# A transformer trunk on one core: the memory's projections begin earlier and run denser in the attention, and the top-k masks are built another way

## The chip, the core and the metric

The kernel runs on one core of one Trainium2 chip. The metric is the device time of one execution in microseconds, the median of several runs. The core has four engines that matter here: TensorE (PE, matrix products and transposes), VectorE (DVE), ScalarE (ACT) and GpSimd (POOL). Each works through its own instructions in a fixed order and waits on semaphores for the others. SyncE (SP) issues all the transfers in one queue.

## What is computed

Two layers of an encoder for 1024 tokens of width 1024. A layer is a mixer (a short convolution, an attention whose keys are picked by an indexer, an attention over a band of chunks), then a cross-attention into 256 memory tokens, then a squared-ReLU MLP, each with a residual and a layer norm.

```
for l in range(DEPTH):                       # 2
    mix = hybrid_mixer(x, positions, w_in[l], conv_w[l], rel_bias[l], w_mix_out[l])
    x = layer_norm(ALPHA * x + mix, ...)
    cross = memory_cross_attention(x, mem, w_mq[l], w_mkv[l], w_mo[l])
    x = layer_norm(ALPHA * x + cross, ...)
    x = layer_norm(ALPHA * x + squared_relu_mlp(x, w_ff1[l], w_ff2[l]), ...)

# in hybrid_mixer, the attention with picked keys (dsa), block of 128 queries:
score = einsum('bqh,bqhs->bqs', iw, relu(einsum('bqhd,bsd->bqhs', iq, ik)))
score = where(admissible, score, -inf)
_, idx = lax.top_k(score, 256)               # ties: the lowest index first
s = where(valid, q . k[idx] * scale, -inf);  out = softmax(s) . v[idx]

# in memory_cross_attention, from mem alone:
k, v = split(einsum('bmd,de->bme', mem, w_kv), 2)
```

## The kernel before

The products are made in three matmuls each, from operands that are split into a high and a low part: `mm3`, lines 340 to 342. A weight unit of 512 columns is loaded by a transfer (line 284), its high part is cast on ACT (285) and its low part subtracted on POOL (286).

A layer has these stages in order of time. First the projections of the token stream and, beside them, the indexer and a bitwise search for each query's 256th largest score (`topk`; line 788 on ACT and 792 on DVE count how many scores exceed a candidate). Then **the attention**: 24 units of the chunk attention (6 heads by 4 pairs of blocks, 48 softmax rows of 128 queries) and 16 units of the dsa attention (8 blocks `b` by 2 halves of the heads, 48 softmax rows). A softmax row's scores are made on PE (line 1088 for chunk, 1220 for dsa, two matmuls a pass), one or two passes of DVE add bias or mask and take the minimum (988), ACT makes the exponential (994), POOL divides (1005), PE transposes (1125, 1240), ACT and DVE split (644, 645), and PE multiplies by the values (1139, 1249). A unit's values come three units behind its scores (`pipeline`, `LEAD = 3`). A dsa unit needs its block's mask, which `masks` makes for blocks 2 to 7; wider blocks have wider rows, up to 1024 keys.

Into the attention three streams are merged (`merge`, at the end of `back`): the units, the mask steps, and `memory`, which computes for the cross-attention what depends on the memory tokens alone: for each of 4 heads the keys, the values, and the values times the output weights (stored to DRAM by line 1412). Per layer that is 384 matmuls of 256 columns and 96 of 512. Each stream advances by numbers that it yields; `after(START, RATE, ...)` delays `memory` to the moment 30 and stretches its steps by 2.0. The attention's units sum to some 158 of these moments, and `memory`'s steps to 62.4 before they are stretched. The order so written is a priority; a scheduler that works with a model of the chip then fixes every engine's order when the program is built.

After the attention comes the output projection (`out_proj`), whose 16 weight units are `w_mix_out`; then the cross-attention, its projection and the MLP.

Of the kernel before, what the change touches and what calls it, by code (L numbers as in the profile page):

```python
# [15 lines left out]
BF16 = mybir.dt.bfloat16  # L16
I32 = mybir.dt.int32
AF = mybir.ActivationFunctionType
ALU = mybir.AluOpType
# [3 lines left out]
S = 1024  # L23
# [9 lines left out]
TOPK = 256  # L33
# [4 lines left out]
BIG = 2.0**100  # L38
# [8 lines left out]
ROOMY = 8192  # L47
FILL = 200
TP = 2.5
START = 30  # L50
RATE = 2.0
EARLY = 0
STEP = 32
STAGES = 4
# [256 lines left out]
class Kern:  # L311
# [508 lines left out]
    def masks(self, st):  # L820

        nc, sb = self.nc, self.sb
        while "found" not in st:
            yield 1.0
        state, col = st.pop("found")
        for g, blocks in list(enumerate(GROUPS))[::-1]:
            fl, cnt = state[g][0], state[g][2]
            for j, b in list(enumerate(blocks))[::-1]:
                w = (b + 1) * P
                sc = st["score"][b]  # L830
                tcol = fl[:, j : j + 1]
                tmp = [sb.alloc(w) for _ in range(2)]
                eq, pre = (x.ap for x in tmp)
                if g == 0:


                    above, more = self.small(1), self.small(1)
                    nc.vector.tensor_scalar(
                        eq, sc.ap, tcol, None, op0=ALU.is_gt, op1=ALU.add,
                        accum_out=cnt[:, j : j + 1],  # L840
                    )
                    nc.vector.tensor_scalar(
                        eq, eq, -HIGH, HIGH, op0=ALU.mult, op1=ALU.add
                    )
                    nc.vector.tensor_tensor_reduce(
                        pre, sc.ap, eq, 1.0, HIGH, op0=ALU.add, op1=ALU.min,
                        accum_out=above,
                    )
                    nc.vector.tensor_scalar(
                        more.bitcast(I32), cnt[:, j : j + 1], float(TOPK), None,  # L850
                        op0=ALU.is_ge,
                    )
                    nc.vector.copy_predicated(tcol, more.bitcast(I32), above)

                nc.vector.tensor_scalar(
                    eq, sc.ap, tcol, BIG, op0=ALU.is_equal, op1=ALU.mult
                )
                nc.vector.tensor_scalar(
                    sc.ap, sc.ap, tcol, None, op0=ALU.is_le, op1=ALU.add,
                    accum_out=cnt[:, j : j + 1],  # L860
                )
                need = self.small(1)
                nc.vector.tensor_scalar(
                    need, cnt[:, j : j + 1], float(TOPK - w), BIG, op0=ALU.add, op1=ALU.mult
                )
                nc.vector.tensor_tensor_scan(pre, eq, eq, 0.0, op0=ALU.add, op1=ALU.max)
                nc.vector.scalar_tensor_tensor(
                    eq, pre, need, eq, op0=ALU.is_le, op1=ALU.mult
                )
                nc.vector.scalar_tensor_tensor(  # L870
                    sc.mask, sc.ap, BIG, eq, op0=ALU.mult, op1=ALU.subtract
                )
                for x in [sc.high] + tmp:
                    sb.free(x, self.w.late)
                st["masks"].add(b)
                yield 7.5
        sb.free(col, self.w.late)
# [1100 lines left out]
    def build(self):  # L1978
# [14 lines left out]
        for l in range(DEPTH):  # L1993
# [16 lines left out]
            def attention():  # L2010
                yield from self.pipeline(units())
                for x in ("dkT", "dv"):
                    sb.free(st.pop(x))

            def back():
# [20 lines left out]
                def mask_steps():  # L2036
                    for d in st["mask steps"]:
                        yield 2.0 * d

                yield from self.merge(  # L2040
                    attention(), mask_steps(),
                    self.after(START, RATE, self.shift(FILL, self.memory(l, st))),
                )
# [99 lines left out]
```

## Time and profile before

| | |
|---|---|
| median of 3 runs | 3014.02 us (3011.82 to 3014.43) |
| profiled execution | 3010.65 us, of which its span is 3008.8 us |
| PE busy in the span | 2884.2 us (96%) |
| DVE, ACT, POOL busy | 2155.3 (72%), 1558.0 (52%), 1299.5 us (43%) |
| attention of layer 1, layer 2 | from 297 to 572 us, from 1786 to 2062 us of the span |

PE's busy time is the union of its matmuls' durations; matmuls overlap in the pipeline, so a busy PE can still do little. The first softmax pass of a layer starts its attention; the last matmul of line 1249 is near its end. Shares of the other engines are true occupancy.

### The profile page before, as it was taken

Reading aid. Unit: us, or ns where it says so; the run is one execution under the profiler, and the core shown is the slowest. Engines: PE = TensorE matmul, PEld = TensorE weight load, DVE = VectorE, ACT = ScalarE, POOL = GpSimd, SP = SyncE. Lnnn points to the kernel's source line nnn. Section 1 sums busy time; section 2 is a strip of 40 time slices with the busy share of each in tenths; the row PEclk is TensorE's granted clock in tenths of the full one; section 3 lists DMA queues with packets and bytes.
Section 4 is the critical chain, followed back from the end, with each engine's and each line's share of the span. In section 5 each row is a group of like instructions: output and inputs, shape, how many; then the busy total and the mean of one; then the engine's idle time right before and its main releaser. Section 6 shows DMA issues by size and latency. Waiting matters only on the chain. (4 is left out here: it accounts for less than half of the span.)

```text
span 3008.8 us, 43448 instructions
## 1 busy us (share of the span) xinstructions
PE 2884.2 (96%) x14440; PEld 2440.8 (81%) x14440; DVE 2155.3 (72%) x4321; ACT 1558.0 (52%) x3146; POOL 1299.5 (43%) x1242
## 2 busy tenths in 40 slices
PE   8999889999999999999999998899999999999998
PEld 7787778788877788888788877887888778888886
DVE  5897786582487766777857987866625877667788
ACT  5676777623234455543457767784222445554432
POOL 4614575522335553222457146653222555532223
PEclk9999999999999999999999999999999999999999
DMA  4213333331334546755422144232213354476553
GB/s 127 63 36 85 101 110 106 105 119 36 114 116 161 171 154 217 255 178 188 131 68 66 37 100 118 92 117 97 93 47 111 112 175 163 152 250 223 189 179 116
DMA packets 264288, 381.99 MB, mean 127 GB/s; under 512 B 23040, under 2 KB 141824, under 8 KB 264064
## 3 DMA queue, kind: packets, MB, share of 16 engines
q1 hardware_dynamic: 264064, 379.22, 38.7%
q8 instruction: 114, 1.87, 0.3%
q14 instruction: 110, 0.90, 0.1%
HBM read 269.56 MB, written 95.42 MB: 121 GB/s over the span
## 5 line engine op out<-in xcount | busy, mean ns | idle before, releaser
L340 PE MATMUL banks<-sb,sb 128*128 128x512 f32 (+3 forms) x3776 | 1423.0, 378 | 19.7 <-DVE sb L645 6.3
L341 PE MATMUL banks<-sb,sb 128*128 128x512 f32 (+3 forms) x3776 | 1417.7, 376 | 8.6 <-POOL sb L286 8.6
L342 PE MATMUL banks<-sb,sb 128*128 128x512 f32 (+3 forms) x3776 | 1413.9, 376 | 7.7 <-POOL sb L645 7.4
L645 POOL TENSOR_TENSOR sb<-sb,sb 128x512 fp32r<-128x512 f32 (+1 forms) x428 | 590.1, 1390 | 931.3 <-ACT sb L644 793.5
L340 PEld LDWEIGHTS banks<-sb,sb 128*128 128x128 f32 x3776 | 714.3, 189 | 151.4 <-DVE sb L645 9.1
L342 PEld LDWEIGHTS banks<-sb,sb 128*128 128x128 f32 x3776 | 712.7, 189 | 133.2 <-POOL sb L645 9.2
L341 PEld LDWEIGHTS banks<-sb,sb 128*128 128x128 f32 x3776 | 714.4, 189 | 130.8 <-POOL sb L286 10.3
L644 ACT CAST sb<-sb 128x512 fp32r<-128x512 f32 (+1 forms) x788 | 452.8, 605 | 583.5 <-PE banks L341 146.2
L286 POOL TENSOR_TENSOR sb<-sb,sb 128x512 fp32r<-128x512 f32 (+2 forms) x288 | 381.4, 1340 | 480.1 <-ACT sb L285 421.2
L645 DVE TENSOR_TENSOR sb<-sb,sb 128x512 fp32r<-128x512 f32 x360 | 273.2, 785 | 43.8 <-ACT sb L644 41.4
L645 DVE TENSOR_TENSOR sb<-banks,sb 128x384 fp32r<-128x384 f32 (+2 forms) x324 | 188.0, 595 | 86.4 <-ACT sb L644 78.9
L285 ACT CAST sb<-sb 128x512 fp32r<-128x512 f32 (+2 forms) x288 | 170.4, 606 | 136.1 <-PE banks L342 30.4
L644 ACT CAST sb<-banks 128x384 fp32r<-128x384 f32 (+2 forms) x324 | 159.7, 517 | 140.5 <-PE banks L1557 75.3
L792 DVE TENSOR_SCALAR_CACHE_REDUCE sb<-sb,sb 128x768 bf16<-128x768 f32 (+3 forms) x256 | 207.5, 810 | 5.0 <-POOL sb L443 2.0
L1721 DVE TENSOR_TENSOR sb<-sb,sb 128x512 f32<-128x512 f32 x160 | 155.5, 1006 | 60.9 <-ACT sb L1701 56.9
L1005 POOL TENSOR_SCALAR sb<-sb,sb 128x128 f32<-128x128 f32 (+7 forms) x192 | 148.2, 786 | 86.4 <-DVE sb L1003 65.9
L1763 DVE TENSOR_TENSOR sb<-banks,sb 128x512 f32<-128x512 f32 x224 | 149.4, 682 | 47.4 <-PE banks L342 45.7
L788 ACT ACTIVATE sb<-sb,sb 128x1024 bf16<-128x1024 f32 (+1 forms) x128 | 140.4, 1097 | 74.2 <-DVE sb L811 64.9
L1826 DVE TENSOR_TENSOR sb<-sb,sb 128x512 f32<-128x512 f32 x128 | 112.8, 882 | 68.4 <-DMA sb<-w_ff_dram 68.0
L994 ACT ACTIVATE sb<-sb,sb 128x128 f32<-128x128 f32 (+7 forms) x192 | 141.6, 739 | 27.9 <-DVE sb L988 26.5
L1700 ACT ACTIVATE sb<-sb 128x512 f32<-128x512 f32 x128 | 80.7, 631 | 117.6 <-DVE sb L1763 117.1
L1333 DVE SCALAR_TENSOR_TENSOR sb<-sb,banks 128x512 f32<-128x512 f32 x64 | 43.4, 685 | 113.2 <-PE banks L342 110.5
(172 smaller groups left out, 3046.9 us busy)
## 6 DMA issues: line engine op xcount, KB each, us to landing
sb<-h SPq DMA_DIRECT2D x236, 256.0 KB, 3.1
h<-sb SPq DMA_DIRECT2D x224, 256.0 KB, 2.2
sb<-w_ff_dram SPq DMA_DIRECT2D x216, 256.0 KB, 3.1
sb<-w_ff_dram SPq DMA_DIRECT2D x64, 512.0 KB, 4.1
sb<-w_in_dram SPq DMA_DIRECT2D x64, 256.0 KB, 2.9
sb<-w_mkv_dram SPq DMA_DIRECT2D x64, 256.0 KB, 2.8
sb<-sb SPq DMA_DIRECT2D x54, 256.0 KB, 3.6
xs<-sb SPq DMA_DIRECT2D x24, 512.0 KB, 2.8
```

What stands on the lines that cost most here:

```text
L285: k.nc.scalar.copy(hi, st)
L286: k.nc.gpsimd.tensor_tensor(lo, st, hi.bitcast(F32), op=ALU.subtract)
L340: mm(out, lh, rh, start=start, stop=False)
L341: mm(out, lh, rl, start=False, stop=False)
L342: mm(out, ll, rh, start=False, stop=stop)
L644: nc.scalar.copy(hi, src)
L645: eng.tensor_tensor(lo, src, hi.bitcast(F32), op=ALU.subtract)
L792: nc.vector.tensor_scalar(junkb[:, :w], x, c, None, op0=ALU.is_ge, op1=ALU.add, accum_out=n)
L994: nc.scalar.activation(pt.ap, pt.ap, AF.Exp, bias=mn, scale=-1.0, accum_out=sm)
L1005: nc.gpsimd.tensor_scalar(pt.ap, pt.ap, rc[:, i : i + 1], 0.0, op0=ALU.mult, op1=ALU.add)
L1721: nc.vector.tensor_tensor(z.ap, x, y, op=ALU.add if spec[1] == "+" else ALU.subtract)
L1763: nc.vector.tensor_tensor(r.ap, ps.ap, part[c, x].ap, op=ALU.add)
```

## The change

Two numbers: `memory` starts at the moment 10 in place of 30, and its steps are stretched by 1.1 in place of 2.0, so it ends at about 79 in place of 155. And the end of `masks`: before, DVE compares the scores for equality and for less-or-equal with the threshold, each over the whole row, scans the equal ones, and combines in two more passes. Now ACT writes the sign of threshold minus score (-1, 0, 1, as bf16, with its sum), DVE compares the sign with zero, scans, and combines in two passes; `need` takes one more instruction on one column.

```
-START = 30
-RATE = 2.0
+START = 10
+RATE = 1.1
...
+                side, same = (eq.bitcast(BF16)[:, i * w : (i + 1) * w] for i in range(2))
+                total, need = self.small(1), self.small(1)
+                nc.scalar.activation(
+                    side, sc.ap, AF.Sign, bias=tcol, scale=-1.0, accum_out=total
+                )
+                nc.vector.tensor_scalar(same, side, 0.0, None, op0=ALU.is_equal)
+                nc.vector.tensor_tensor_scan(pre, same, same, 0.0, op0=ALU.add, op1=ALU.max)
+
                 nc.vector.tensor_scalar(
-                    eq, sc.ap, tcol, BIG, op0=ALU.is_equal, op1=ALU.mult
+                    need, pre[:, w - 1 : w], total, 0.5, op0=ALU.add, op1=ALU.mult
+                )
+                nc.vector.tensor_scalar(need, need, float(TOPK - w // 2), None, op0=ALU.add)
+                nc.vector.scalar_tensor_tensor(
+                    pre, side, 4.0 * S, pre, op0=ALU.mult, op1=ALU.add
                 )
                 nc.vector.tensor_scalar(
-                    sc.ap, sc.ap, tcol, None, op0=ALU.is_le, op1=ALU.add,
-                    accum_out=cnt[:, j : j + 1],
-                )
-                need = self.small(1)
-                nc.vector.tensor_scalar(
-                    need, cnt[:, j : j + 1], float(TOPK - w), BIG, op0=ALU.add, op1=ALU.mult
-                )
-                nc.vector.tensor_tensor_scan(pre, eq, eq, 0.0, op0=ALU.add, op1=ALU.max)
-                nc.vector.scalar_tensor_tensor(
-                    eq, pre, need, eq, op0=ALU.is_le, op1=ALU.mult
-                )
-                nc.vector.scalar_tensor_tensor(
-                    sc.mask, sc.ap, BIG, eq, op0=ALU.mult, op1=ALU.subtract
+                    sc.mask, pre, need, BIG, op0=ALU.is_gt, op1=ALU.mult
                 )
```

What that does to the order is seen at three places. PE, layer 1, chunk attention: the place of the first projection matmuls of `memory` (340 to 342, 256 columns) among score passes (1088). Before, they stand behind 84 matmuls of line 1088:

```order
L1088 MATMUL banks<-sb_2839,sb_2815 128x320
L1088 MATMUL banks<-sb_2839,sb_2817 128x320
L340 MATMUL banks<-sb_331,sb_652 128x256
L341 MATMUL banks<-sb_2629,sb_652 128x256
L342 MATMUL banks<-sb_331,sb_652 128x256
```

Now they stand behind 38 of them:

```order
L1088 MATMUL banks<-sb_2620,sb_2608 128x320
L1088 MATMUL banks<-sb_2620,sb_2610 128x320
L1139 MATMUL banks<-sb_2919,sb_2629 128x256
L1139 MATMUL banks<-sb_2919,sb_2629 128x128
L340 MATMUL banks<-sb_2816,sb_652 128x256
L341 MATMUL banks<-sb_2818,sb_652 128x256
L342 MATMUL banks<-sb_2816,sb_652 128x256
```

So the projections begin with the twentieth score pass in place of the forty-third. PE, layer 2, dsa attention, block 5 (scores 1220, transposes 1240, values 1249), with `memory`'s products of 512 columns among them before:

```order
L1220 MATMUL banks<-sb_2610,sb_16370 128x384 x2
L1249 MATMUL banks<-sb_3450,sb_2608 128x384
L340 MATMUL banks<-sb_1821,sb_2813 128x512
L341 MATMUL banks<-sb_1821,sb_2813 128x512
L342 MATMUL banks<-sb_1821,sb_2813 128x512
L340 MATMUL banks<-sb_629,sb_2813 128x512
L341 MATMUL banks<-sb_629,sb_2813 128x512
L342 MATMUL banks<-sb_629,sb_2813 128x512
L1220 MATMUL banks<-sb_2610,sb_16370 128x384 x2
L1249 MATMUL banks<-sb_16732,sb_2608 128x384
```

The same place now:

```order
L1220 MATMUL banks<-sb_2610,sb_16887 128x384 x2
L1249 MATMUL banks<-sb_2762,sb_2620 128x384
L1220 MATMUL banks<-sb_2610,sb_16696 128x384 x2
L1249 MATMUL banks<-sb_5505,sb_2620 128x384
L1249 MATMUL banks<-sb_5399,sb_2620 128x384
L1249 MATMUL banks<-sb_5204,sb_2620 128x384
L1249 MATMUL banks<-sb_17042,sb_2620 128x384
L1220 MATMUL banks<-sb_2610,sb_16696 128x384 x2
```

No projection matmul is left among the scores and values. Counted over the program, of the 480 projection matmuls of a layer's `memory`, 240 (layer 1) and 246 (layer 2) stand behind the 60th softmax row before (192 of 256 columns, 48 and 54 of 512), and none now. POOL, end of layer 2's attention: the last divisions (1005), then weight units of the output projection (286) and splits of the attention's result (645). Before:

```order
L1005 TENSOR_SCALAR sb_4126<-sb_4126,sb_2662 128x1024
L1005 TENSOR_SCALAR sb_1671<-sb_1671,sb_2662 128x1024
L286 TENSOR_TENSOR sb_666<-sb_97,sb_666 128x512
L645 TENSOR_TENSOR sb_5639<-sb_14346,sb_5656 128x512
L645 TENSOR_TENSOR sb_5639<-sb_1761,sb_5656 128x512
L286 TENSOR_TENSOR sb_1837<-sb_102,sb_1837 128x512
L645 TENSOR_TENSOR sb_5639<-sb_16340,sb_5656 128x512 x2
```

Now:

```order
L1005 TENSOR_SCALAR sb_1761<-sb_1761,sb_2662 128x1024
L1005 TENSOR_SCALAR sb_163<-sb_163,sb_2662 128x1024
L286 TENSOR_TENSOR sb_2618<-sb_97,sb_2618 128x512
L286 TENSOR_TENSOR sb_2818<-sb_102,sb_2818 128x512
L286 TENSOR_TENSOR sb_659<-sb_107,sb_659 128x512
L286 TENSOR_TENSOR sb_652<-sb_112,sb_652 128x512
L286 TENSOR_TENSOR sb_317<-sb_97,sb_317 128x512
```

Eight weight units of the output projection now stand right behind the last division, where one stood before the first split.

## Rows read from the trace of the kernel before

**Rows 1.** The page, part 1: busy time and share of the span of one engine.
```profile
PE 2884.2 (96%) x14440; PEld 2440.8 (81%) x14440; DVE 2155.3 (72%) x4321; ACT 1558.0 (52%) x3146; POOL 1299.5 (43%) x1242
```

In the rows of stretches the columns are: stretch (us from the start of the span), its length, busy time of PE, PEld (weight loads), DVE, ACT and POOL with the number of instructions, PEclk (the clock granted to TensorE as a share of its full speed), the busy share of the transfer engines, GB/s. Rows of one line alone show only the engines that run it.

**Rows 2.** Busy us of each engine (count) in stretches of attention; columns below.
```profile
296.90:443.40 146.50, 127.49 (x851) 114.45 (x851) 118.09 (x339) 106.19 (x259) 89.23 (x102) 0.92 0.38 107
443.40:529.30 85.90, 84.20 (x570) 75.44 (x569) 60.30 (x170) 69.47 (x159) 52.97 (x62) 1.00 0.34 109
529.30:572.00 42.70, 40.00 (x234) 33.61 (x233) 32.57 (x72) 35.51 (x74) 15.08 (x13) 1.00 0.23 78
1785.70:1929.90 144.20, 126.55 (x848) 112.94 (x848) 118.93 (x335) 105.98 (x261) 92.73 (x105) 0.93 0.39 108
1929.90:2019.20 89.30, 85.28 (x583) 77.59 (x581) 63.75 (x176) 71.55 (x160) 54.54 (x61) 1.00 0.35 112
2019.20:2062.00 42.80, 37.30 (x210) 30.07 (x209) 33.13 (x75) 34.06 (x71) 17.61 (x15) 0.96 0.22 77
```

**Rows 3.** TensorE in order of time, consecutive projection matmuls: start, duration.
```profile
506.40 0.28 PE L341 MATMUL banks<-sb,sb 128*128 128x256 f32 x1
506.52 0.28 PE L342 MATMUL banks<-sb,sb 128*128 128x256 f32 x1
```

**Rows 4.** All engines in two stretches without a projection matmul.
```profile
300.00:350.00 50.00, 41.70 (x253) 36.95 (x254) 44.83 (x136) 38.60 (x94) 26.01 (x35) 0.86 0.31 91
2025.00:2040.00 15.00, 13.53 (x77) 10.56 (x75) 11.82 (x31) 13.03 (x27) 7.08 (x6) 1.00 0.05 19
```

**Rows 5.** The score passes, line 988 alone, in chosen stretches: VectorE busy, count.
```profile
300.00:350.00 50.00, 17.16 (x70) 0.86 0.31 91
350.00:420.00 70.00, 16.87 (x66) 0.98 0.46 127
440.00:520.00 80.00, 24.81 (x86) 1.00 0.36 115
1790.00:1835.00 45.00, 15.71 (x64) 0.92 0.36 100
1835.00:1905.00 70.00, 16.01 (x64) 0.98 0.44 122
1945.00:2025.00 80.00, 25.32 (x84) 1.00 0.38 123
2025.00:2040.00 15.00, 6.36 (x18) 1.00 0.05 19
```

**Rows 6.** One of the three projection lines, 340, in the same stretches.
```profile
350.00:420.00 70.00, 21.64 (x71) 13.55 (x72) 0.98 0.46 127
440.00:520.00 80.00, 24.62 (x79) 15.06 (x79) 1.00 0.36 115
1835.00:1905.00 70.00, 22.88 (x74) 14.02 (x74) 0.98 0.44 122
1945.00:2025.00 80.00, 24.07 (x76) 14.36 (x76) 1.00 0.38 123
```

**Rows 7.** The page, part 5: casts of weight units on ACT: busy, mean ns.
```profile
L285 ACT CAST sb<-sb 128x512 fp32r<-128x512 f32 (+2 forms) x288 | 170.4, 606 | 136.1 <-PE banks L342 30.4
```

**Rows 8.** Lines of the mask and one of the search: count, min/median/max in ns.
```profile
L855 DVE TENSOR_SCALAR sb<-sb,sb x12: 420/626/1159, 267.9 to 1925.7; 128x384 f32<-128x384 f32 x2, 128x512 f32<-128x512 f32 x2, 128x640 f32<-128x640 f32 x2, 128x768 f32<-128x768 f32 x2
L858 DVE TENSOR_SCALAR_CACHE_REDUCE sb<-sb,sb x12: 603/936/1279, 268.7 to 1926.5; 128x384 f32<-128x384 f32 x2, 128x512 f32<-128x512 f32 x2, 128x640 f32<-128x640 f32 x2, 128x768 f32<-128x768 f32 x2
L863 DVE TENSOR_SCALAR sb<-sb x12: 126/140/154, 270.2 to 1931.5; 128x1 f32<-128x1 f32 x12
L870 DVE SCALAR_TENSOR_TENSOR sb<-sb,sb x12: 557/940/2649, 271.0 to 1936.2; 128x384 bf16<-128x384 f32 x2, 128x512 bf16<-128x512 f32 x2, 128x640 bf16<-128x640 f32 x2, 128x768 bf16<-128x768 f32 x2
L788 ACT ACTIVATE sb<-sb,sb x128: 1026/1098/1155, 145.6 to 1774.0; 128x1024 bf16<-128x1024 f32 x64, 128x896 bf16<-128x896 f32 x64
```

**Rows 9.** All engines where attention hands over to the output projection.
```profile
585.00:590.00 5.00, 2.72 (x12) 1.91 (x11) 0.00 (x0) 1.14 (x2) 5.00 (x5) 1.00 0.10 36
2060.00:2065.00 5.00, 4.24 (x10) 3.37 (x11) 3.05 (x5) 5.00 (x11) 2.90 (x3) 0.50 0.21 82
```


## Prediction

> **What bounds the kernel now.** I read the page first [rows 1]: PE is busy 2884 of 3009 us, so 125 us are visibly idle, and every other engine has room over the whole span. A share over the span hides the stages, so I read the stretches of the attention next, the only place where the change touches the order strongly [rows 2]. I cut each layer at the 60th softmax row, the last row of dsa block 1. Ahead of the cut (called C: chunk attention and the two narrow dsa blocks) a layer takes 146.5 and 144.2 us. Behind it (called D: dsa blocks 2 to 7 to the last product) it takes 85.9 + 42.7 = 128.6 and 89.3 + 42.8 = 132.1 us. In C the fullest engines are PE (127 of 146) and DVE (118), and PE's granted clock is 0.92; in D, PE (84 of 86) and ACT (69). PE's busy time deceives here: a projection matmul of 256 columns counts 0.28 us of busy time, but the next begins 0.12 us behind its start [rows 3]. So the attention is bound by no single engine for long; DVE leads where no projection runs (44.83 of 50 us [rows 4]), PE where they run.
>
> What matters for a change that moves projections is their price: what one costs in time in either place. The score passes (line 988) are the measure of progress [rows 5], and lines 340 to 342 count the projections; 341 and 342 have as many as 340 within one, so a stretch's count is three times that of 340 [rows 6].
>
> - Layer 1, no projections: 70 passes in 50 us, 1.40 a us. With 3 x 71 = 213: 66 passes in 70 us. Without, 66 passes take 47.1 us. So 213 cost 22.9 us: 0.107 us each.
> - Layer 2: 64 in 45 us, 1.42 a us; with 3 x 74 = 222, 64 in 70 us, which would be 45.0. So 222 cost 25.0 us: 0.113 each.
> - In D, rows differ in width, so I take DVE's time in the passes. Without projections (layer 2, the end): 6.36 in 15 us, 0.424. With them 24.81 and 25.32 us of passes take 80 us where 58.5 and 59.7 would do: 21.5 us for 3 x 79 = 237, and 20.3 for 3 x 76 = 228; 0.091 and 0.089 each.
>
> The price in C is near PE's pitch of 0.12 us, although without projections PE starts only 253 matmuls in 50 us there, 5.1 a us [rows 4], against 6.5 in D (570 + 583 in 175.2 us [rows 2]). That is the main thing to see: a projection isn't hidden in either place, it is nearly paid for.
>
> **The change, part by part.**
>
> *The move.* 240 and 246 matmuls go from D to C. C pays 240 x 0.107 = 25.7 and 246 x 0.113 = 27.8 us, 26.7 on average. Its bounds: those that now stand among rows 8 to 24 (156 in layer 1, 120 in layer 2, counted in the order) might fill PE's gaps for nothing, which takes off 156 x 0.107 = 16.7 and 120 x 0.113 = 13.6, so 11.5; or all cost their full pitch, 192 x 0.12 plus 48 at twice that by width, 34 us. I take the middle, since measured prices are from C itself. ACT doesn't become C's bound: half of the 48 casts of weight units go along, and with them half of the 24 copies that empty banks, all of 512 columns, 36 x 0.61 = 22 us [rows 7]. With its 106 us [rows 2] and 6 for the signs ACT stands at 134 of some 172 us, since C grows as well.
>
> D gets back 240 x 0.090 = 21.6 us at the measured price. The most that it can get back: DVE has 60.3 + 32.6 = 93 us of work in D [rows 2], nearly all of which stays (some 90 without the projections' splits and a last mask); at the best share seen without projections, 0.90 [rows 4], D takes 100, so it saves 28.6. I take 24.8, between the two, since D's end from which the price comes has the widest rows alone. Here DVE is what is late next, then ACT (105 us less some 22, of about 104). Move: 26.7 - 24.8 = 1.9 slower a layer, +4 in all; ends from -34 (11.5 against 28.6) to +25 (34 against 21.6).
>
> *Masks.* Six a layer. Gone: the equality pass (0.626 us at the median), the less-or-equal pass (0.936); the last pass (0.940) becomes a plain compare and multiply, whose nearest rows are these two, 0.626 to 0.940 [rows 8]; the scan and the pass ahead of the last stay. New on DVE: a compare of the bf16 signs, between nothing and 0.626 (I take 0.4: same form as the equality pass, narrower data), and one instruction on a column, 0.14 by line 863 [rows 8]. Saved: 0.626 + 0.936 + 0.940 - (0.80 + 0.40 + 0.14) = 1.16 us a mask, 7 a layer (5 to 10). The Trainium skill, VectorE: DVE Perf Modes, section "The perf-mode tier table", gives 693 ns for 2048 bf16 elements of such an instruction, so by it, as an estimate, a mean row of 704 costs 0.24 us, and a layer saves 1 us more; no row of before shows the form. New on ACT: a sign over the row, in form the search's line 788, 1.10 us at 960 columns on average; 0.81 when scaled to 704; with the readout of its sum I take 1.0, so 6 us a layer [rows 8]. Neither is all on the path: masks are made in C, where from now on projections fill PE. I count a third of DVE's 7 as gained and a sixth of ACT's 6 as lost: -1.5 a layer, -3 in all (ends -14 to +12 for both layers: one of the two wholly on the path).
>
> *The handover.* PE waited 2.3 us for POOL's weight subtraction (585 to 590, POOL full 5.00 of 5.00), and in layer 2 stood at 10 matmuls in 5 us at half clock (0.50) [rows 9]. With POOL free in D, eight weight units stand right behind the last division. I count 2 us a layer: -4 (0 to -10).
>
> *The clock.* In the first 50 us PE was granted 0.86 [rows 4]; its matmuls there end late, but DVE at 44.83 of 50 hides most of it. With projections from the twentieth pass on the clock should hold: -1 a layer, -2 (0 to -6).
>
> Transfers: the 48 weight loads a layer and 16 stores of products are the same ones; on SP's queue they now pass the head pairs' copies (line 1019). Transfer engines are 0.38 busy in C [rows 2], which covers it; without that cover each copy that comes late costs a wait like those seen, some 2 us.
>
> Sum against the profiled execution: 3010.65 + 4 - 3 - 4 - 2 = 3005.65. The median of the runs is 3.4 us above that execution, which gives **3009 us**.
>
> **Rivals.**
>
> 1. *D doesn't pick up* (ends slower). In static order, three units deep, the dsa units may be held by the chain from DVE to ACT to POOL to PE, and PE, at 5.1 matmuls a us in place of 6.5, may lose its full clock as it did at the start of C (0.86 [rows 4]). If D gets back half, 12.4 us, the sum is 3010.65 + 2 x (26.7 - 12.4) - 9 = 3030, by the median 3034. It decides below 19 us a layer: 2 x (26.7 - 18.9) - 9 is +6. Against it: 2025 to 2040, without projections, holds 1.00. The Trainium skill, Perfetto Trace Analysis, section "Optimization Strategy", says that regimes with different most-contended engines gain from being interleaved; here PE's regime is taken out of D, whose next engine is DVE, and put into C alone. By that rule the time comes out as this rival's; the equal prices of the rows don't bear it out so far.
> 2. *C hides it.* The first 156 and 120 are free: 2 x (11.5 - 24.8) - 9 = -36, by the median 2978. For it: before 350 us PE starts 5.1 matmuls a us, not 6.5; against it, the 0.107 and 0.113 come from stretches with gaps too.
> 3. *The signs hurt.* ACT's 6 us a layer delay exponentials and DVE's saving lies under PE: +12 in place of -3: 3024. Against it: ACT's 106 of 146 in C.
> 4. *Nothing moves* beyond 6 us: equal prices, small terms cancel.
>
> **How the numbers follow.** My forecast, 2997 to 3021, gets 0.46 with the fourth rival in it; the second 0.20, the first 0.22, the third 0.12. About 0.2%, 6 us, is what a measurement of this kernel can tell from no change. The forecast splits into faster 0.22, same 0.22, slower 0.02; so faster 0.42, same 0.22, slower 0.36. The range reaches from the second rival to a little over the first, 2978 to 3036; outside are the ends where several bounds add.
>
> **What would show it.** C should last 165 to 175 us with PE's clock near 1.00; D 100 to 108 with DVE above 0.85 and no line 340 until the output projection; passes with projections at about 0.94 a us in all of C from the twentieth on. Line 860 should take under 0.6 us and line 857 about 1 us. POOL's full stretch after the attention should shrink and the 2.3 us wait be gone. I am wrong if D stays over 110 us, or if C lasts under 160.

## The result and the profile after

The changed kernel took 3032.67 us (median of 4 runs, 3027.31 to 3036.89), the kernel before 3014.22 in the runs beside it (3011.82 to 3018.95): ratio 1.0056, 95% interval [1.0039, 1.0074]. It is slower by 0.6%, more than the 0.2% that this measurement can tell from no change. The forecast of 3009 us had the wrong sign; the range 2978 to 3036 holds the time.

The profiled execution of after took 3036.89 us and spans 3035.1, 26.3 more than before. Its stretches, cut as in [rows 2] (C, then D in two pieces, for each layer; columns as there):

```profile
297.90:476.30 178.40, 158.25 (x1104) 144.00 (x1103) 125.40 (x336) 131.00 (x306) 117.26 (x124) 0.96 0.48 137
476.30:538.00 61.70, 57.27 (x345) 45.36 (x344) 57.05 (x174) 54.98 (x132) 26.75 (x41) 1.00 0.06 17
538.00:575.00 37.00, 34.82 (x203) 28.70 (x203) 29.43 (x66) 27.83 (x58) 18.21 (x15) 1.00 0.29 93
...
1793.40:1986.00 192.60, 166.15 (x1108) 149.55 (x1107) 122.42 (x338) 133.75 (x311) 122.76 (x130) 0.93 0.45 132
1986.00:2045.00 59.00, 53.73 (x326) 43.27 (x326) 55.37 (x166) 51.55 (x125) 25.11 (x38) 1.00 0.05 15
2045.00:2086.00 41.00, 36.22 (x206) 28.59 (x204) 30.74 (x71) 35.08 (x74) 24.59 (x21) 0.98 0.19 65
```

The reader sees two opposite movements. D went from 128.6 and 132.1 us to 61.7 + 37.0 = 98.7 and 59.0 + 41.0 = 100.0: 62.0 us won, and DVE fills 57.05 of 61.7 and 55.37 of 59 there. C went from 146.5 and 144.2 to 178.4 and 192.6: 80.3 us lost. All else lost 8.0. 80.3 - 62.0 + 8.0 is the 26.3. D's end is a choice, since the output projection's matmuls stand among the last ones of line 1249: cut behind the last of these (577.0 and 2059.6 us in before, 587.2 and 2082.7 in after), D wins 22.7 and 33.0, 55.7 in all, and all else loses 1.7; cut at the first pass of the last softmax row, D wins 26.3 and 36.3. C's loss is the same by every cut.

The price of a projection in C, read as in [rows 5, 6]: line 988's passes and line 340's matmuls in the same stretches of after. First the passes (DVE busy, count):

```profile
300.00:350.00 50.00, 13.98 (x56) 0.97 0.48 125
350.00:476.00 126.00, 24.98 (x106) 0.96 0.46 138
1795.00:1835.00 40.00, 10.91 (x42) 0.87 0.39 109
1835.00:1986.00 151.00, 28.24 (x120) 0.94 0.47 138
```

Then line 340 (PE, PEld):

```profile
300.00:350.00 50.00, 11.85 (x38) 7.21 (x38) 0.97 0.48 125
350.00:476.00 126.00, 40.20 (x122) 23.97 (x122) 0.96 0.46 138
1795.00:1835.00 40.00, 5.10 (x17) 3.53 (x17) 0.87 0.39 109
1835.00:1986.00 151.00, 47.03 (x144) 28.33 (x143) 0.94 0.47 138
```

The counts of line 988, here and in [rows 5], hold two instructions for each score pass, the pass and the readout of its accumulator: C has 84 passes and some 168 of these.

```profile
L988 DVE DVE_READ_ACCUMULATOR2_ANT sb<- x288: 73/83/90, 298.5 to 2060.2; 128x1 f32 x144
```

There are 288 passes in both layers, and 288 readouts. So a rate of 1.40 "passes" a us is 0.70 in truth; the prices below and in the prediction stand all the same, since both sides of each are counted alike, and the text goes on counting so.

By the prediction's own reading, at 1.40 passes a us, 106 passes need 75.7 us, so the 366 projections of the second stretch cost 50.3 us, 0.137 each; in layer 2, at 1.42, 120 passes need 84.5 and 432 projections cost 66.5, 0.154 each. In before it was 0.107 and 0.113. The rate there is 106 in 126 us and 120 in 151, 0.84 and 0.79 a us, where the prediction expected 0.94.

The masks' new lines (counts, min/median/max ns):

```profile
L857 ACT ACTIVATE sb<-sb,sb x12: 600/884/1149, 268.4 to 1950.8; 128x384 bf16<-128x384 f32 x2, 128x512 bf16<-128x512 f32 x2, 128x640 bf16<-128x640 f32 x2, 128x768 bf16<-128x768 f32 x2
L857 ACT ACTIVATION_READ_ACCUMULATOR sb<-sb,sb x12: 185/189/200, 268.9 to 1951.9; 128x1 f32 x12
...
L860 DVE TENSOR_SCALAR sb<-sb x12: 259/374/1422, 269.1 to 1952.1; 128x384 bf16<-128x384 bf16 x2, 128x512 bf16<-128x512 bf16 x2, 128x640 bf16<-128x640 bf16 x2, 128x768 bf16<-128x768 bf16 x2
...
L866 DVE TENSOR_SCALAR sb<-sb x12: 129/150/155, 270.6 to 1957.0; 128x1 f32<-128x1 f32 x12
...
L870 DVE TENSOR_SCALAR sb<-sb,sb x12: 407/898/1596, 271.3 to 1958.7; 128x384 bf16<-128x384 f32 x2, 128x512 bf16<-128x512 f32 x2, 128x640 bf16<-128x640 f32 x2, 128x768 bf16<-128x768 f32 x2
```

And the handover, where [rows 9] had PE waiting:

```profile
585.00:590.00 5.00, 5.00 (x24) 4.12 (x23) 0.55 (x1) 3.95 (x8) 4.74 (x5) 1.00 0.36 116
2080.00:2085.00 5.00, 2.35 (x7) 1.26 (x8) 1.84 (x4) 4.98 (x11) 5.00 (x5) 0.94 0.29 104
```

In layer 1 the wait is gone: PE starts 24 matmuls in place of 12, and from 575 to 625 us it waits for no POOL. In layer 2 PE stands at 7 in 5 us beside a full POOL and a full ACT; its waits there, from 2078 on, are for ACT (2.1 us for line 644, 0.8 for 285).

### The profile page after: what moved, and what is told of

It reads as the page before. It is cut to its first block, busy times and chain, and to the rows that moved or that the text cites. A ratio compares the mean times of both kernels' runs of the same rounds, so it can differ in the third digit from the quotient of the medians.

```text
span 3035.1 us, 43475 instructions
## 1 busy us (share of the span) xinstructions
PE 2897.9 (95%) x14440; PEld 2442.3 (80%) x14440; DVE 2162.1 (71%) x4309; ACT 1569.1 (52%) x3170; POOL 1299.0 (43%) x1242
## 5 line engine op out<-in xcount | busy, mean ns | idle before, releaser
L645 DVE TENSOR_TENSOR sb<-sb,sb 128x512 fp32r<-128x512 f32 x360 | 287.3, 824 | 43.9 <-ACT sb L644 43.9
L988 DVE CUSTOM_DVE_ANT_0 sb<-banks,sb 128x128 f32<-128x128 f32 (+5 forms) x192 | 96.7, 509 | 46.5 <-PE banks L1088 27.0
```

Source lines behind the costliest of these rows:

```text
L645: eng.tensor_tensor(lo, src, hi.bitcast(F32), op=ALU.subtract)
```

## Experiments

All diffs are against the changed kernel, "after" below. Softmax rows are counted from 0: C is the stretch from the first score pass to that of row 60, the first of dsa block 2, as above, layer 1 / layer 2; after has 178.4 / 192.6, before 146.5 / 144.2. Rows 60 to 95 are the rest, up to the first pass of row 95. Ratios are to the kernel before, with a 95% interval. Expectations call the reasons that they set against each other theories, by a letter.

### Which half of the change costs

**masks_only**: the old start and rate, the new masks.

```
-START = 10
-RATE = 1.1
+START = 30
+RATE = 2.0
```

> The new masks with the old numbers (30 and 2.0). Theory A, that the loss is the move of the projections into the chunk attention, expects this kernel within 0.3% of before, 3008 to 3020 us, and the same lengths of C (146.5 and 144.2 us) and D within 4 us. Theory B, that the signs on ScalarE delay the exponentials, expects most of the loss here: over 3024 us, with C longer by 8 us or more in each layer.

3010.75 us, ratio 0.9988 [0.998, 0.9997]: 3.6 us faster, as the sum's -3. C 138.6 / 144.0:

```profile
297.90:436.50 138.60, 124.57 (x846) 110.72 (x846) 113.95 (x334) 111.10 (x271) 90.12 (x104) 0.93 0.40 113
1785.50:1929.50 144.00, 125.00 (x843) 111.80 (x842) 112.46 (x327) 110.57 (x269) 87.22 (x105) 0.93 0.40 110
```

The masks aren't the loss.

**sched_only**: the new start and rate (10, 1.1), the masks of before (the kernel before with the two numbers changed).

> The new numbers (10 and 1.1) with the old masks. Theory A expects the whole loss here, 3026 to 3040 us, C at 178 us or more in both layers, D near 100. Theory B expects at most 3020 us. If the new masks in truth save time on VectorE in C, this kernel is slower than the changed one by some 5 us.

3041.81 us, ratio 1.009 [1.0077, 1.0103]; C 174.9 / 202.7. The move alone costs 27 us, the whole loss and more.

### How the price depends on how many are moved

**start30_rate11** (START 30, RATE 1.1) and **start60** (START 60, RATE 1.5), both with the new masks. By the program's order 360 and 348 projection matmuls then stand ahead of row 60 in the first, 114 and 114 in the second; 228 and 222 in masks_only and before, 480 in after. (Counted so, up to the first scores of block 2, the change moves 252 and 258; the count in "The change", 240 and 246, starts 12 matmuls later.)

> New masks, the old start (30) with the new density (1.1): 360 and 348 projection matmuls stand ahead of row 60, against 228 and 222 before and 480 in the changed kernel. Theory A with a price that rises with density (0.14 to 0.15 us each in C against 0.09 in D) expects 130 x 0.05 = 6 us a layer or more, 3022 to 3032 us. If it is the early start that costs, not the density, it stays within 3010 to 3018 us.

3014.24 us, 0.9998 [0.9989, 1.0008]; C 165.5 / 164.1, rows 60 to 95 86.7 / 90.4. The time alone would speak for the early start as the cost, and not the density. But C and the later rows are together 16.2 us longer than in masks_only, and what lies outside them is 14 shorter (2506 against 2520 us), where both kernels do the same work: the time hides the price.

> New masks, start 60, stretch 1.5: 114 projection matmuls are left ahead of row 60 and 342 or more stand behind it. If a projection is dearer in C than in D at any density (0.11 against 0.09), C gives back 114 x 0.11 = 12.5 us and D pays 102 x 0.09 = 9: some 3 us a layer less than before, 3006 to 3012 us. If D then becomes bound by TensorE, each costs its pitch there (0.14): 3014 to 3024 us.

3010.65 us, 0.9987 [0.9977, 0.9996]; C 134.6 / 132.5, rows 60 to 95 113.5 / 114.6.

With masks_only (138.6 / 144.0; 100.0 / 107.9) and after (178.4 / 192.6; 73.4 / 71.3) between and beyond, the price of one more matmul in C is the difference in length over the difference in count. From 114 to 228 it is 4.0 / 114 = 0.04 us in layer 1 and 11.5 / 108 = 0.11 in layer 2; from there to 360 and 348 it is 26.9 / 132 = 0.20 and 20.1 / 126 = 0.16; from there to 480 it is 12.9 / 120 = 0.11 and 28.5 / 132 = 0.22. What the later part gives back for each is flatter: 0.12 and 0.06, 0.10 and 0.14, 0.11 and 0.14. Up to half of the projections the two are about even (15.5 us for C, 20.2 for the later rows); beyond, C pays 88.4 us and the later rows return 63.2. Single steps are less sure: start45 below shows C and the later rows moving by some 10 us without a reason in the counts, which is 0.08 us a matmul on a step of 120.

**start45** (START 45, RATE 1.75, new masks) lies between two settings of equal time.

> New masks, start 45 and rate 1.75: between the two settings that both took 3010.65 to 3010.75. From the prices measured on the way (0.03 to 0.11 us a matmul moved out of the chunk attention, 0.07 to 0.13 us for each that the later part takes) both theories expect 3006 to 3012 us; a gain of more than 5 us would speak for an optimum between the two.

3020.53 us, 1.0024 [1.0014, 1.0034]: slower than both neighbours by 10 us, which neither theory said. C has 133.7 / 145.6, rows 60 to 95 have 112.3 / 105.5. Against masks_only C is 3 us shorter and the later rows 10 longer; against start60 C is 12 longer and the later rows 10 shorter; what lies outside is 4 and 7 us longer, where this kernel does the same work. No single place has the loss, and no run tells its cause.

### What is late in C: queues and blocks

In after's C the transfer queue SP and PE wait for these, among others (in all, times, longest; layer 1):

```profile
SPq L284 <- POOL sb L286: 66.9, 34, 7.7
SPq L1412 <- ACT sb L1409: 24.4, 11, 4.5
SPq L1019 <- DMA sb<-sb: 11.7, 6, 3.5
```

```profile
PE banks L1088 <- DMA sb<-sb: 7.8, 2, 6.4
PE banks L1088 <- DVE sb L988: 4.6, 5, 2.0
PE banks L340 <- ACT sb L1409: 3.7, 5, 1.2
```

Line 284 is the load of a weight piece, which waits for POOL to be done with the landing buffer; the stores of products (1412) wait for ACT; behind them in SP's queue stand the copies of head pairs (1019), for which PE's line 1088 waits. In layer 1's C of before SP waited 49.5, 12.4 and 9.8 us at these three places, and PE not at all for the copies. So I moved either off SP.

```
-                    nc.sync.dma_start(
+                    nc.scalar.dma_start(
                         self.values[r : r + P, d * 512 : d * 512 + 512], o.ap
```

> The changed kernel with the 16 stores a layer of the products (line 1412) issued by ScalarE right behind the copy that they store, not by SyncE; SyncE's queue waited some 25 us a layer in C for those copies. TensorE's order in layer 2 is almost the same as in the changed kernel. Theory Q expects C shorter by 5 to 10 us a layer, 3015 to 3025 us; theory P expects 3028 to 3038 us.

3039.86 us, 1.0092 [1.0067, 1.0117]; C 180.6 / 190.9. In **copies_actq** the copies of line 1019 are issued by ACT in the same way.

> The changed kernel with the head pairs' 27 copies a layer (line 1019) issued by ScalarE, so that they don't stand behind weight loads that wait for GpSimd (67 and 74 us of waiting in C in the changed kernel). Theory Q expects C shorter by 8 us or more a layer, under 3024 us, unless ScalarE is held up by the copies' own waits; theory P expects 3028 to 3040 us.

3038.3 us, 1.0088 [1.0067, 1.0109]; C 178.5 / 194.6. SP's order alone isn't the price.

**fine_units** hands the mk and mv projections out twelve matmuls at a time, not forty-eight:

```
                     self.w.done(i)
+                    yield 1.3
...
-            ps = project("mk")
+            ps = yield from project("mk")
...
```

> The changed kernel, but a projection of 48 matmuls gives way to the other streams after every 12 of them in place of after all 48 (the same work in all). Theory P, that blocks of projections in TensorE's fixed order hold up the attention's own matmuls and drain its chain, expects C shorter by 8 us or more a layer, 3012 to 3024 us. Theory Q, that transfers come late because one queue carries weights, stores and the attention's copies, expects no change: 3028 to 3038 us.

3026.54 us, 1.0047 [1.0031, 1.0063]; C 179.4 / 176.8: 16 us less in layer 2's C, nothing in layer 1's, and 10 us lost outside rows 0 to 95. That lies between the two theories' times. **masks_fine** is the same at START 30 and RATE 2.0.

> New masks, start 30 and rate 2.0 as in the kernel before, projections handed out twelve matmuls at a time in place of forty-eight. Theory P: the blocks cost something here too, 1 to 5 us back: 3006 to 3010 us. Theory S: no change, within 2 us of 3010.8.

3042.6 us, 1.0097 [1.0081, 1.0114]: 32 us slower than masks_only where at most 5 us of gain were expected. C 148.1 / 150.2, rows 60 to 95 105.2 / 110.1, each a little longer. A bank of PSUM is held through four handouts in place of one; whether that is why, no run tells.

### What is late in C: room

As a rule the program gives a tile the on-chip columns that have been free longest. With the early start the memory's buffers are taken earlier, so fewer are free while C runs. **stages8** takes 2048 columns away (STAGES 8, four more landing buffers of weights).

> The changed kernel with 8 buffers for arriving weights in place of 4 (2048 columns more of on-chip memory). Theory Q in its other half, that SyncE stands still until GpSimd has freed a buffer, expects the queue's wait for line 286 to fall by half and C to be shorter by 5 us or more a layer: 3015 to 3026 us. If buffers for the attention itself are what is short in C, the 2048 columns less make it slower: over 3036 us. Theory P expects 3028 to 3038 us.

3100.57 us, 1.0289 [1.0265, 1.0313]; C 204.0 / 185.1. But by the trace 45 of the 62 us over after lie outside rows 0 to 95. So the next two take 1024 columns for the attention alone.

```
+                dead = sb.alloc(1024, top=True)
                 yield from self.merge(
                     attention(), mask_steps(),
...
+                sb.free(dead)
```

> The changed kernel with 1024 columns of on-chip memory that nobody uses, taken from the start of the attention to its end. Theory S (room): the chunk attention, where the memory's buffers now stand from row 10 on, loses 15 to 60 us in the two layers together: 3048 to 3093 us. Theory P (matmuls in PE's order): within 6 us of the changed kernel's 3032.7.

3050.86 us, 1.0126 [1.0108, 1.0144]: 18 us over after; C 179.0 / 207.9.

> The same 1024 dead columns in the kernel with the new masks alone, whose projections begin thirty units in. Theory S: room is less short, so a loss under a third of the one in the changed kernel: 3011 to 3025 us. Theory P: within 6 us of 3010.8. If it loses as much as the changed kernel does, room is scarce in both and the early start is not what makes it so.

3029.22 us, 1.0049 [1.0033, 1.0064]: 18 us over masks_only as well; C 145.4 / 148.0. In time, less room costs the late start as much as the early one (in C 15.9 us of the early one and 10.8 of the late), which speaks against scarcity as what the early start adds.

**roomy_after** gives 3584 columns back; its values are those of the later of two writes.

```
-        mt = [[sb.alloc(4 * MEM) for _ in range(2)] for _ in range(2)]
+        mt = [[sb.alloc(4 * MEM)] * 2 for _ in range(2)]
...
-        st["mk"] = [sb.alloc(512, top=True) for _ in range(4)]
+        st["mk"] = [sb.alloc(512, top=True)] * 4
...
```

> The changed kernel with the memory's two pairs of transposed buffers laid on one pair and the four kept results on one buffer (3584 columns of on-chip memory given back, all instructions stay, the values are of the later write). Theory S: the chunk attention loses at least half of what it gained in length, to 150 to 170 us a layer, time 2990 to 3015 us. Theory E: the queues are as full as before, within 6 us of 3032.7.

3048.47 us, 1.0112 [1.0098, 1.0126]; C 1.5 us longer over both layers, as good as unchanged:

```profile
299.10:480.00 180.90, 159.06 (x1104) 145.21 (x1104) 124.27 (x337) 133.38 (x312) 119.32 (x128) 0.95 0.47 139
1794.70:1986.30 191.60, 161.45 (x1098) 146.40 (x1097) 121.38 (x336) 134.00 (x312) 123.31 (x131) 0.93 0.44 129
```

Theory S, too little room, falls: with 3584 columns given back, C is as long as in after. The time, 16 us over after, was expected by neither theory. **masks_stages3** (STAGES 3, 512 columns more, otherwise masks_only) asked the same of the late start.

> New masks, start 30 and rate 2.0 as before, three landing buffers for weights in place of four (512 columns given back in the whole program). Theory S: 1024 columns fewer cost 18 us in this kernel, so 512 more give 3 to 9 us: 3002 to 3008 us. Theory E: the same or slower, since a load waits sooner for its landing buffer: 3010 to 3020 us.

3038.97 us, 1.0081 [1.0067, 1.0095]: 28 us slower than masks_only, the opposite of S; but it also has one landing buffer fewer, for which a load can wait, so it doesn't tell room from that.

### What is late in C: the work that comes along

**one_pass** leaves out 256 of a layer's 480 matmuls, with all else in place:

```
-                        self.mm3(
+                        nc.tensor.matmul(
                             ps.ap[:, f * MEM : (f + 1) * MEM],
-                            hi[:, k4 * P : (k4 + 1) * P], lo[:, k4 * P : (k4 + 1) * P],
-                            mv[0][g][:, k4, :], mv[1][g][:, k4, :], k == 0, k == NK - 1,
+                            hi[:, k4 * P : (k4 + 1) * P],
+                            mv[0][g][:, k4, :], start=k == 0, stop=k == NK - 1,
```

> Left out: in the mk and mv projections of the memory two of the three matmuls of each split product (256 of 480 a layer); every buffer, transfer, split and the order of all else stay as in the changed kernel. If the matmuls themselves make the price of the chunk attention (theory P: PE's time and its fixed order with blocks of projections), 224 matmuls should cost there about what the 228 of the kernel with the new masks alone cost: chunk attention 139 to 150 us a layer in place of 178 and 193, time 2945 to 2970 us. If the buffers that the memory takes early make it (theory S: shortage of on-chip room), the chunk attention stays over 165 us a layer and the time at 2995 us or more.

3026.82 us, 1.0045 [1.003, 1.006]. **noconv** keeps the matmuls and the loads, and leaves out ACT's and POOL's conversions of the memory's weights, 48 pieces a layer (96 in the two). The matmuls read another operand and the pieces land past the landing buffers, so PE's waits for these weights, and SP's for POOL to free a landing buffer for them, go with the conversions:

```
-        k.nc.sync.dma_start(v, src)
-        k.nc.scalar.copy(hi, st)
-        k.nc.gpsimd.tensor_tensor(lo, st, hi.bitcast(F32), op=ALU.subtract)
+        if self.emitted in self.raw:
+            st = k.sb.tensor(hl.off, 1016, F32)[:, :n]
+            v = st if len(dims) == 1 else st.rearrange("p (a b) -> p a b", a=dims[0])
+            k.nc.sync.dma_start(v, src)
+        else:
...
```

> Left out of the changed kernel: the conversion of the memory's 96 weight pieces a layer (ScalarE's copy of 619 ns and GpSimd's difference of 1379 ns each); the pieces are still loaded into buffers of the same size at the same places of the program, and all 480 matmuls run, on another operand. Theory E (the price of the chunk attention is the side work on ScalarE and GpSimd, which comes along with the projections and stands in the attention's queues): the chunk attention falls to 145 to 160 us a layer from 178 and 193, time 2975 to 3005 us. Theory S (buffers): the buffers are taken as early as before, the chunk attention stays over 168 us a layer, time 3015 us or more.

3028.4 us, 1.0046 [1.0032, 1.0059]. Taken alone, either of these two runs came out as the theory of buffers had it. **both_out** leaves out both.

> Left out of the changed kernel together: two of the three matmuls of each split product of the mk and mv projections (256 of 480 a layer) and the conversion of the memory's 96 weight pieces a layer; loads, buffers, stores and their places stay. If two limits of like height stand side by side, TensorE's work and the side work of ScalarE and GpSimd, so that taking one away only uncovers the other: chunk attention 140 to 158 us a layer and 2960 to 2995 us. If it is the loads and buffers and the waits on them: chunk attention over 165 us a layer in both, 3010 us or more.

3008.67 us, 0.9984 [0.9975, 0.9994]. **bare** leaves out the memory's weights wholly: loads, buffers, conversions, and 448 of 480 matmuls, as its code has it (16 of either width stay; the expectation says 416).

> As the run before, and the memory's weights left out wholly: no loads, no weight buffers, 416 of the 480 matmuls gone; the transposes, the kept results, the copies, splits and stores stay at their places. The floor of the chunk attention with the early start: 125 to 140 us a layer by either reading, 2940 to 2975 us. If it stays over 160 us a layer, nothing that the memory does on an engine makes the price, and the order of the attention itself does.

2932.81 us, 0.9724 [0.971, 0.9739]. C of the four, layer 1 and 2; one_pass:

```profile
299.30:472.40 173.10, 140.29 (x847) 122.62 (x847) 126.62 (x339) 131.07 (x307) 121.88 (x124) 0.88 0.50 141
1789.30:1979.30 190.00, 148.51 (x854) 127.21 (x852) 124.17 (x338) 134.21 (x311) 123.17 (x130) 0.87 0.45 134
```

noconv:

```profile
296.00:471.00 175.00, 155.53 (x1103) 144.98 (x1103) 114.15 (x336) 108.47 (x262) 60.11 (x82) 0.95 0.49 140
1789.20:1976.60 187.40, 164.52 (x1108) 149.02 (x1107) 118.85 (x338) 111.31 (x266) 58.82 (x86) 0.93 0.48 136
```

both_out:

```profile
298.30:458.80 160.50, 134.24 (x848) 118.92 (x848) 114.44 (x336) 108.89 (x263) 58.22 (x82) 0.91 0.54 154
1775.70:1954.40 178.70, 142.47 (x852) 126.01 (x851) 118.36 (x338) 110.51 (x266) 57.57 (x86) 0.86 0.50 142
```

bare:

```profile
294.00:421.60 127.60, 105.60 (x650) 90.01 (x649) 111.37 (x334) 105.06 (x260) 59.21 (x81) 0.91 0.32 93
...
1739.20:1864.00 124.80, 104.44 (x654) 89.93 (x655) 111.04 (x331) 102.38 (x257) 50.81 (x78) 0.91 0.33 92
```

Over both layers C has 371.0 us in after, 363.1 without the matmuls (-7.9), 362.4 without the conversions (-8.6), 339.2 without both (-31.8, about twice the sum of the two), 252.4 in bare (-118.6). By layer the pair gives 17.9 where the single runs add up to 8.7, and 13.9 where they add up to 7.8. That fits two limits side by side, PE's work and the conversions on ACT and POOL: take one away and the other, with the loads, still sets C. In one_pass POOL's 122 of 173 us stay, and the granted clock goes from 0.96 to 0.88; in noconv PE stays 155 of 175 busy. It isn't proved by size: the 15 us that the pair gives over its parts are less than C's spread over the kernels that start early (last section).

Nor are these two the whole price. Each C of both_out has 224 projection matmuls, about as many as masks_only's 228 and 222, and none of the memory's conversions; still it is 160.5 and 178.7 us long against 138.6 and 144.0. By its expectation both_out lies between the two readings, and its time, 3008.67, is just short of that of loads, buffers and waits (3010 or more). What it has more of than masks_only is what comes along with the other 256 matmuls: 44 weight loads in layer 1's C against 26, and their buffers, bank copies and stores. Of the 87 us between both_out and bare, the 192 matmuls a layer that go there too would fill 64 at their pitch, as an estimate (112 of 256 columns at 0.12 us [rows 3], 80 of 512 at 0.23 by their starts in before's trace). That is no price: at its pitch one_pass took away 61 us and gained 7.9. So the loads and weight buffers and the waits on them are worth some 23 us of the 87 or more, which no run takes apart further. The time from a load's issue to its landing isn't the reason by itself: its median is 2.7 us in after's C of layer 1 and 2.9 in masks_only's.

## Why the prediction was wrong, point by point

**The step that failed** is "C pays 240 x 0.107 = 25.7 and 246 x 0.113 = 27.8 us", with its reason, "I take the middle, since measured prices are from C itself", and its upper end of 34. C got 31.9 and 48.4 us longer with the masks' saving in it, 39.8 and 48.6 against masks_only: 80.3 and 88.4 for the two layers where 53.4 stood in the sum. The price was off in two ways. It was read against 1.40 passes a us, the speed of C's first stretch. Bare has the score passes (its line 996) almost without projections over all of C:

```profile
294.00:345.00 51.00, 18.39 (x74) 0.90 0.36 101
345.00:421.60 76.60, 21.92 (x95) 0.91 0.29 87
1739.20:1786.00 46.80, 18.16 (x73) 0.86 0.31 85
1786.00:1864.00 78.00, 22.06 (x98) 0.93 0.34 97
```

In the later part they go at 95 / 76.6 = 1.24 and 98 / 78 = 1.26 a us without being held by projections. Against that, the 66 passes of [rows 5] need 53.2 us, and the 213 projections cost 16.8, 0.079 each; in layer 2 the 222 cost 0.086; in after, the same reading gives (126 - 85.5) / 366 = 0.111 and (151 - 95.2) / 432 = 0.129. So the average price in before was even lower than I read it. But it was an average, and I used it for the next ones: a matmul more cost 39.8 / 252 = 0.16 and 48.6 / 258 = 0.19 us. The first ones were cheap: masks_only's C has 196 and 190 projection matmuls more than bare's and is 11.0 and 19.2 us longer, roughly 0.06 and 0.10 each, loads and conversions included. In before the projections stood in a bunch of 66 or 64 passes, and some 100 passes of C had next to none; in after none of C's later part is without them, 366 on 106 passes and 432 on 120.

Why the next ones are dearer is shown only in part. A projection brings conversions, copies, loads and buffers along; the pair of removals fits conversions and PE's work both standing at C's height, so that either alone keeps C long. But with both cut back to about masks_only's number or below, C stays 56.6 us longer than masks_only's, of 88.4 in all: most of the price lies with the rest that comes along or with the order, and its cause stays open. I had set ACT's 134 us against 172 and concluded that "ACT doesn't become C's bound". As a sum that held (131.00 of 178.40, 133.75 of 192.60), but 0.73 and 0.69 of a stretch were no free room: without ACT's and POOL's conversions the cut of the matmuls gave 23 us (362.4 to 339.2) where it gave 8 with them.

**D's term held in its mechanism**, and was too small. I took 24.8 a layer, with 28.6 as the most; D gave 29.9 and 32.1. DVE is what was late next, as the prediction said: its share is 0.92 and 0.94 in D's first piece, 0.88 and 0.86 over all of D, its work there 86.5 and 86.1 us in place of 90. By the other two cuts of D the mean of the layers is 27.9 and 31.3, so the upper end was nearer than the halfway value by any of them; the 28.6 was worked out from layer 1's 128.6 alone. So the first rival, that D doesn't pick up, is wrong in its mechanism, although its 3034 us is close to the time; that is luck, and the range holds the time only because it reaches a little beyond that rival. Neither sign of being wrong that the prediction named came true, since none asked for a C longer than 175 us. The Trainium skill, Perfetto Trace Analysis, section "Optimization Strategy", which speaks for interleaving regimes with different most-contended engines, gave the right sign; what was lost lay in C, and not in D, where I had looked for it. The same section says that recurring gaps can mean too little SBUF or PSUM for the next tile. Here less room did cost time (18 us for 1024 columns), but 3584 columns more gave C nothing.

**The masks** held: 3.6 us won alone, against 3; on top of the move (after against sched_only) it is 9.1 us, and the scatter told of in the last section is as wide. Line 860 took 374 ns at the median where I took 0.4 us, line 857 with its readout 884 + 189 ns against 1.0 us, line 870 898 ns against 0.8. The Trainium skill, VectorE: DVE Perf Modes, section "The perf-mode tier table", gave, as an estimate, 0.24 us for a mean row; the trace has 0.13 more, and is still far under the 0.626 of the old equality pass on 32-bit data. The third rival, that the signs hurt, is wrong.

**The handover and the clock** gave nothing. The 2.3 us wait of layer 1 went, as forecast; yet the stretches outside C and D got 8.0 us longer in all (1.0 ahead, 4.7 between, 2.3 behind; 1.7 in all with D cut behind its last product), where the sum had -4. C's clock went from 0.92 to 0.96 in layer 1 and stayed at 0.93 in layer 2; "near 1.00" was wrong.

**The second rival**, that the first 156 and 120 matmuls are free, is wrong: 114 in the first 50 us cost 10 us (56 passes, 40 us at 1.40), 0.088 each, and 51 in 40 us of layer 2 cost 10.4, 0.20 each.

Sum by what was measured: C +80.3 in place of +53.4, D -62.0 in place of -49.6, all else +8.0 in place of -4 -2; the masks' -3 lies in C and D.

**No version is much faster.** masks_only and start60 beat the kernel before by 0.12 and 0.13%, within what counts as no change.

## What to carry to other kernels

The price of a filler, read where it stands now, is an average of the first ones, and it hangs on the speed that one takes for the stretch without it; for moving more in, look at two densities, or allow for more than the pitch of the fullest engine (here 0.16 and 0.19 us at a pitch of 0.12), since side work comes along (conversions, copies, loads). A limit that a removal doesn't show may stand beside another: take both away before you rule either out. And read what the stretch that is emptied can win from the engine that is late next there; that was nearer to what D gave than a value halfway down from it.

## What was not expected of the hardware and the program

Rearrangements that move hardly any work changed the time by more than the sum's terms. With the new masks and about the old start, six settings took 3010.65 (start60), 3014.24 (start30_rate11), 3020.53 (start45), 3029.22 (dead_masks), 3038.97 (masks_stages3) and 3042.6 us (masks_fine), against 3010.75; giving back 512 columns, with a landing buffer, cost 28 us, and giving back 3584 in after cost 16, of which C had 1.5. A new order gives later tiles other columns, and differences stand in the whole program: the stretches outside rows 0 to 95 of both layers add up to 2506 us in start30_rate11 and 2530 in masks_stages3. By these six, half the spread is 16 us, and a forecast for a reordering of this program needs about that much width for it alone. The longer C is clear of it: over both layers C took 267 to 298 us in the seven kernels that start late with all work (with start30_rate11, the denser one, 330), and 356 to 389 in the eight that start early. Then, a stretch whose matmuls were cut by a quarter (1104 to 847) had its clock granted at 0.88 in place of 0.96; whether that took back a part of what was left out, no run tells.
